# Output projection of an encoder block as seven block products, with sums of the weights kept in DRAM

## The chip, the cores and the metric

The kernel runs on one core of one Trainium2 chip. The metric is device time in microseconds of one execution. TensorE is called PE, VectorE DVE, ScalarE ACT, GpSimd POOL, and SP is the engine that issues most transfers.

## What is computed

The reference is one layer of an encoder with 1024 tokens of width 1024 in float32:

```python
h = jnp.einsum('bsd,de->bse', x, w_in[layer])
q_a, k_a, v_a, z_a, q_b, k_b, v_b, z_b = jnp.split(h, SPLIT_POINTS, axis=-1)
y_a = neighborhood_attention(q_a, k_a, v_a, rel_pos_bias[layer])   # 8 heads of 64, window 8 x 16 in a 16 x 64 grid
qb, kb = rotary(q_b, positions), rotary(k_b, positions)
y_b = windowed_gqa_with_sink(qb, kb, v_b, sink_logits[layer])      # 8 query heads, 2 of keys, |i - j| <= 128
mixed = jnp.concatenate([y_a * jax.nn.silu(z_a), y_b * jax.nn.silu(z_b)], axis=-1)
y = jnp.einsum('bse,ed->bsd', mixed, w_out[layer])
x = layer_norm(DEEPNORM_ALPHA * x + y, ln_gain[layer], ln_bias[layer])
```

(The splitting into heads is left out.) The output projection, `y`, is a product of 1024 x 1024 by 1024 x 1024.

## The kernel before

**Arithmetic.** Products are made in float16 with each operand split in a high and a low part: three passes, high x high, high x low and low x high, are summed in float32 in one PSUM bank of 128 x 512. A split costs a cast on ACT (high part) and a subtraction on DVE or POOL (low part), for weights also a scaling.

**Stages.** First the values are projected, then six of the 21 blocks of 128 columns of the first projection (`project`, L362, with its matmuls at L381). A counter of these matmuls (`run_to`, L390) triggers events at given counts, such as the scans `sum_w` (L700) that read weights for their scale. Then come 128 units of attention, 64 of group b and 64 of group a, one per step. In step i `stage_qk` makes the logits (L799, L800), DVE adds the mask or bias (L809), ACT makes the exponentials (L823) and the high part (L831), DVE the low part (L832), and SP issues a transpose by DMA of both parts (L835). For every four units `stage_pv` multiplies with the values (L861), some steps later. `stage_on` divides, `stage_ot` transposes on PE (L882) and multiplies into the gate `z` (L885, L888). The other 15 projections are fed between the units by `pump_to` (L896) according to the list `FILL_AT`, and after them the first part of the output projection (`out_head`, L1014), 60 matmuls long.

**The order of the work** is the order of the Python calls on each engine: what is written from L571 to L1227 is under a manual schedule. Side work goes through four queues, `enq` and `pop` (L149, L161), one list per engine. In each step `pop` takes a few operations whose inputs were issued in an earlier step (three steps earlier, if the input is a transfer), by priority and then by age: one or more from the list of SP, one or two from ACT's and DVE's, two from POOL's. `need` issues an operation at once if a unit needs it. What follows in `final` (L1025) is ordered by the framework's planner.

**The output projection.** `wo` is loaded in 16 blocks of 128 x 512 (`wo_load`), six of them twice. Every block is scanned for its size in the attention (`wo_scan`: ten on DVE, L939, six on ACT, L936), `wo_scale` (L945) makes one scale, `wo_split` (L955) the parts: eight blocks in the attention, the others in `final`. The gated activations `z` of four of the eight inner blocks (group b) are split by `m_queue` in the attention, the other four in `final`. `out_mms` (L998) makes 3 matmuls per inner block into one bank. `final` first runs what of the second half of row tiles 0 to 2 is ready, then the last four inner blocks for eight banks, then tile by tile. `residual` (L1049) adds a bank to the scaled x (`x_load`, L1043) and gathers statistics, `norm` (L1097) normalizes: one half of the columns on DVE (L1102, L1105), the other on ACT and POOL (L1104, L1107, L1108). The last tile is cut in 256 + 128 + 128 columns and ends in `norm_last` (L1078).

## Time and profile before

| | |
|---|---|
| median of three runs | 447.97 us (447.36 to 450.59) |
| profiled execution | 447.86 us, of which 446.1 us are its span |
| mean granted clock of TensorE | 0.996 |
| busy PE / DVE / ACT / POOL | 438.3 / 346.8 / 302.6 / 211.7 us |
| HBM read / written | 41.19 / 6.32 MB |

Busy times are sums over the whole span; the stages differ. Ends of matmuls are modelled, so that the distance between the starts of matmuls says more than their busy time. In the timeline a row gives the start, the time covered, the engine, the line and what is written from what; in the groups a row gives count, busy time, mean ns of one, and the idle time of the engine before. In the waits a row gives who waited for whom, for how long in total, how often, and the longest. A row of the chain of work gives start, length and what worked.

### The profile page before, as it was taken

The numbers are of one execution on the slowest core, as the hardware profiler recorded it, in microseconds if no ns is written. First come the engines' busy times: TensorE is split into PE (matmuls) and PEld (weight loads), VectorE is DVE, ScalarE is ACT, GpSimd is POOL, SyncE is SP. The second block draws the span as 40 slices with busy tenths as digits, with TensorE's granted clock in tenths as the row PEclk, the third lists the DMA queues.
The fourth block names the chain that finished last, engine by engine and source line by source line (L and its number), as shares of the span: only waits on it lengthen the run. The fifth ranks groups of instructions, "written<-read, shape, count | busy, mean of one in ns | idle before, by whom it ended". The sixth has DMA issues, their size and how long they took to land.

```text
span 446.1 us, 9265 instructions
## 1 busy us (share of the span) xinstructions
PE 438.3 (98%) x3241; PEld 254.7 (57%) x3241; DVE 346.8 (78%) x842; ACT 302.6 (68%) x636; POOL 211.7 (47%) x227
## 2 busy tenths in 40 slices
PE   9999999999999999999999999999999999999995
PEld 8997754444445565655564655555555654444454
DVE  5988867429986797898988887888877737679945
ACT  5849789666599988886867777777777847012411
POOL 0110074636939558767505656655642404304740
PEclk9999999999999999999999999999999999999998
DMA  7921569991149999586876769569569588102711
GB/s 266 391 94 60 164 222 325 278 307 54 48 118 221 188 202 181 95 159 135 168 109 126 144 130 169 112 135 184 116 110 242 108 185 318 48 1 92 238 72 71
DMA packets 123983, 71.20 MB, mean 160 GB/s; under 512 B 96800, under 2 KB 105888, under 8 KB 123936
## 3 DMA queue, kind: packets, MB, share of 16 engines
q1 hardware_dynamic: 123792, 70.48, 65.6%
q8 instruction: 25, 0.41, 0.4%
q14 instruction: 22, 0.18, 0.1%
q10 hardware_dynamic: 144, 0.13, 0.1%
HBM read 41.19 MB, written 6.32 MB: 107 GB/s over the span
## 4 chain that ended last, share of the span: by engine, by line
PE 82%; ACT 5%; DVE 4%; DMA 4%; issue 3%; POOL 1%; SPq 0%; DVEq 0%; POOLq 0%; ACTq 0%
PE ps_pj L381 36%; PE ps_s L1008 9%; PE ps_s L488 6%; PE ps_t L861 6%; PE ps_pj L1008 5%; PE ps_t L1008 5%; PE ps_s L799 3%; PE ps_s L800 3%; PE ps_pj L488 3%; PE ps_t L488 3%; DMA vd<-vt 2%; DMA ws<-in_wt 2%; ACT split L831 1%; PE ps_t L882 1%; DVE qs L257 1%
## 5 line engine op out<-in xcount | busy, mean ns | idle before, releaser
L381 PE MATMUL ps_pj<-xf,wh 128*128 128x512 f16 x672 | 201.3, 379 | 0.9 <-DVE ks L257 0.5
L381 PE MATMUL ps_pj<-xf,wl 128*128 128x512 f16 x336 | 127.3, 379 | 0.0
L381 PEld LDWEIGHTS <-wh 128*128 128x128 f16 x672 | 63.4, 98 | 61.9 <-DVE ks L257 1.3
L823 ACT ACTIVATE ps_s<-sn,nm 128x385 f32<-128x385 f32 (+3 forms) x128 | 70.9, 554 | 29.0 <-DVE nm L809 28.6
L832 DVE SCALAR_TENSOR_TENSOR split<-ps_s,split 128x384 f16<-128x384 f32 (+1 forms) x128 | 66.8, 522 | 30.1 <-ACT split L831 28.4
L1008 PEld LDWEIGHTS <-m 128*128 128x128 f16 x432 | 40.0, 98 | 41.2 <-DVE m L916 0.3
L831 ACT ACTIVATE split<-ps_s 128x384 f16<-128x384 f32 (+1 forms) x128 | 58.6, 458 | 2.4
L381 PEld LDWEIGHTS <-wl 128*128 128x128 f16 x336 | 32.9, 98 | 38.3
L198 POOL TENSOR_SCALAR wr<-wr,wsc 128x512 f32<-128x512 f32 x26 | 20.5, 790 | 66.6 <-ACT wh L193 54.4
L809 DVE CUSTOM_DVE_ANT_0 sn<-ps_s,bm,nsk 128x384 f32<-128x384 f32 (+1 forms) x64 | 40.7, 635 | 0.8 <-PE ps_s L800 0.6
L1008 PE MATMUL ps_s<-wo,m 128*128 128x512 f16 (+1 forms) x192 | 40.7, 366 | 0.0
L799 PE MATMUL ps_s<-ks,qs 128*128 128x384 f16 (+2 forms) x128 | 39.7, 310 | 0.1
L800 PE MATMUL ps_s<-ks,qs 128*128 128x384 f16 (+2 forms) x128 | 39.7, 310 | 0.0
L809 DVE CUSTOM_DVE_ANT_0 sn<-ps_s,bias,sg 128x368 f32<-128x368 f32 (+1 forms) x64 | 36.2, 565 | 3.8 <-PE ps_s L800 3.2
L861 PEld LDWEIGHTS <-tr 128*128 128x128 f16 (+1 forms) x1056 | 36.2, 98 | 2.4
L199 POOL TENSOR_TENSOR wl<-wr,wh 128x512 f16<-128x512 f32 x26 | 32.7, 1256 | 2.2
L299 POOL COPY ks<-ks 64x512 f16<-64x512 f16 x40 | 26.2, 663 | 13.8 <-ACT ks L251 5.2
L1008 PE MATMUL ps_pj<-wo,m 128*128 128x512 f16 (+1 forms) x144 | 26.5, 326 | 0.0
L1107 POOL TENSOR_TENSOR xr<-xr,gb 128x512 f32<-128x512 f32 x7 | 9.8, 1398 | 32.5 <-ACT xr L1104 32.5
L1008 PE MATMUL ps_t<-wo,m 128*128 128x512 f16 x96 | 22.8, 379 | 0.0
L488 PEld LDWEIGHTS <-xf 128*128 128x128 f16 x192 | 18.6, 98 | 7.2
L800 PEld LDWEIGHTS <-qs 128*128 128x128 f16 x128 | 12.5, 98 | 15.5 <-issue 0.8
(190 smaller groups left out, 783.6 us busy)
## 6 DMA issues: line engine op xcount, KB each, us to landing
ws<-in_wt SPq DMA_DIRECT2D x15, 512.0 KB, 6.9
wr<-in_wt SPq DMA_DIRECT2D x26, 256.0 KB, 3.5
wor<-in_wo SPq DMA_DIRECT2D x22, 256.0 KB, 3.3
xr<-in_x SPq DMA_DIRECT2D x8, 512.0 KB, 8.7
out<-xr SPq DMA_DIRECT2D x15, 256.0 KB, 2.0
bias<-in_bias SPq DMA_DIRECT2D x8, 440.0 KB, 3.9
wvraw<-in_wv SPq DMA_DIRECT2D x9, 320.0 KB, 5.8
xraw<-in_xT SPq DMA_DIRECT2D x11, 256.0 KB, 4.4
```

The source lines that it names most:

```text
L199: nc.gpsimd.tensor_sub(l, raw, h)
L299: nc.gpsimd.tensor_copy(place(t, o, half, col), place(t, a, half, col))
L381: nc.tensor.matmul(ps, a[:, k % 4, :], mv, start=(k == 0 and i == 0), stop=(k == KT - 1 and i == 2))
L488: nc.tensor.matmul(ps[:, :320], lh[:, ts], rh[:, cs], start=(k == ko[0] and i == 0), stop=(k == ko[-1] and i == 2))
L799: nc.tensor.matmul(ps[:, :n], q, sl[0], start=True, stop=False)
L800: nc.tensor.matmul(ps[:, :n], q, sl[1], start=False, stop=True)
L809: nc.vector.tensor_tensor_reduce(sn[:, :n], ps[:, :n], bias_t, sg[:, c:c + 1], init, op0=ALU.add, op1=ALU.min, accum_out=nm)
L823: nc.scalar.activation(pt[:, :m], sn[:, :m], AF.Exp, bias=nm, scale=-1.0, accum_out=acc)
L831: nc.scalar.activation(hl[:, :m, 0, :], src, AF.Copy, scale=PSCALE)
L832: nc.vector.scalar_tensor_tensor(hl[:, :m, 1, :], src, PSCALE, hl[:, :m, 0, :], op0=ALU.mult, op1=ALU.subtract)
L861: nc.tensor.matmul(ps[:, w * m:w * m + e], a, b_, start=(i == 0), stop=(i == len(mms) - 1))
L1008: nc.tensor.matmul(ps, lh[:, ts], rh[:, cs], start=(e == EO[0] and i == 0), stop=(e == EO[-1] and i == 2))
```

## The change

The projection is cut in two by two blocks: rows of tokens, inner dimension and columns, each in halves of 512. Seven products of such blocks, q1 to q7 (q4 is called p4), replace the eight. Their left operands are A11, A12, A22 and four sums S1 to S4 of blocks of the gated activations, their right operands B11, B21, B22 and four sums T1 to T4 of blocks of `wo`.

- The scans of `wo` and its scale move from the attention to the loop that projects the values (loads) and to the events of the first six projections (scans and scale).
- `t_prep`, four times in the attention, loads four blocks of `wo` at once, makes T1 to T4, splits them and stores both parts in DRAM (`td`). `t_load` reads them back in `final`. B11, B21 and B22 are loaded, scaled and split as before.
- `m_queue` now splits A11 and S3, the new `m_rest` A12, A22, S1, S2 and S4, for three of the four inner blocks in the attention and for the last in `final`.
- A product is added to banks that already hold another one: q6, q7 and p4 go on top of q1, q3 on top of q5. Between two products `add` adds the bank, with sign + or -, to x (31 additions for 18).
- The list that fills the attention has 57 matmuls of the projection for 60.
- `norm` of all tiles but the last goes through ACT for all 1024 columns and through POOL for gain and bias. All eight tiles of x have a buffer.
- `final` stands under the manual schedule too.

The diff, cut to its core:

```diff
-MSCALE = 2.0 ** -44
+MSCALE = 2.0 ** -46
-LTT, LPP, BH, ND, NA, NX, F1 = 1, 6, 9, 1, 1, 6, 0.2
+LTT, LPP, BH, ND, NA, NX, F1 = 1, 6, 9, 1, 1, 8, 0.2
...
-WO_TAG = ("wor", "wor", "raw", "raw") + ("wr",) * 5 + ("wor", "wor", "raw", "raw", "raw", "wr", "wr")
-WO_SCAN = ((9, 2), (12, 4), (10, 6), (13, 8), (14, 10), (15, 13))
-WO_PREV = {15: ("s", 9), 0: ("s", 10), 1: ("s", 15), 2: ("s", 12), 3: ("s", 13), 11: ("s", 14)}
-WO_SCALE = 55
 M_AT = [105, 112, 118, 120]
-WO_AT = [67, 71, 75, 79, 84, 88, 93, 98]
-WO_LD = [16, 22, 19, 25, 36, 39, 42, 45, 48, 112, 116, 28, 130, 130, 130, 130]
+T_AT = [2, 27, 52, 77]
+B_LD = [36, 39, 42, 45, 48, 70, 78, 87]
+B_AT = [67, 71, 75, 79, 84, 88, 93, 98]
+L_LD = [112, 115, 118, 121]
+L_AT = [126, 128, 130, 132]
+H_AT = [122, 124, 126]
...
+    td = dram.tile([4, 128, 4, 1024], F16, name="td")
...
+        def wo_scan_load(k):
+            for b, w in ((2 * k, "h"), (2 * k + 1, "l")):
+                scans[b] = vw.tile([128, 512], F32, tag=f"wv{w}{k}", name=f"wos{b}")
+                nc.sync.dma_start(scans[b], wo[b // 4, :, b % 4])
+
+        def wo_scan(b):
+            t, m = scans.pop(b), wom[:, b:b + 1]
+            if b % 3 == 2:
+                nc.scalar.activation(t, t, AF.Abs, accum_out=m)
+            else:
+                nc.vector.tensor_reduce(m, t, axis=AXX, op=ALU.add, apply_absolute_value=True)
+
+        def wo_scale():
+            ps = bank("t")
+            nc.tensor.matmul(ps[:, :16], ones, wom.bitcast(BF16)[:, 1::2], start=True, stop=True)
+            nc.vector.tensor_reduce(wog, ps[:, :16], axis=AXX, op=ALU.max)
...
+            nc.vector.tensor_scalar_mul(wos, wos, 0.25)
+            for i in range(2):
+                nc.vector.tensor_scalar(yc[:, i:i + 1], wog, mc, (4.0, -4.0)[i], op0=ALU.mult, op1=ALU.mult)
...
+            wo_scan_load(i)
...
+        for b in range(16):
+            at(18 + 5 * b, wo_scan, b)
         at(219, w_scale, NPRO)
+        at(225, wo_scale)
...
-    rawp = ctx.enter_context(tc.tile_pool(name="rawp", bufs=3, reuse_waits="tile"))
+    rawp = ctx.enter_context(tc.tile_pool(name="rawp", bufs=1, reuse_waits="tile"))
...
-    FILL_N = [48] * len(FILL) + [9, 9, 6, 12, 24]
+    FILL_N = [48] * len(FILL) + [9, 9, 6, 12, 21]
...
+    part, done = {}, {}
+    LHS = {"q1": "A11", "q2": "A12", "q3": "S4", "p4": "A22", "q5": "S1", "q6": "S2", "q7": "S3"}
+    RHS = {"q1": "B11", "q2": "B21", "q3": "B22", "p4": "T4", "q5": "T1", "q6": "T2", "q7": "T3"}
+    ZL, ZH = slice(0, 512), slice(512, S)
+
+    def pair_of(t, *keys):
+        for n, key in enumerate(keys):
+            part[key] = t[:, n, 0, :], t[:, n, 1, :]
...
+    def t_prep(i):
+        raw, hl = {}, {}
+
+        def load():
+            raw[0] = rawp.tile([128, 4, 512], F32, tag="raw", name=f"wor{i}")
+            nc.sync.dma_start(raw[0], wo[i])
+
+        def scale(b):
+            nc.gpsimd.tensor_scalar(raw[0][:, b], raw[0][:, b], wos, 1.0, op0=ALU.mult, op1=ALU.mult)
+
+        def combine(o, fn, a, b):
+            return lambda: getattr(nc.gpsimd, fn)(raw[0][:, o], raw[0][:, a], raw[0][:, b])
+
+        def hi(n, b):
+            if n % 2 == 0:
+                hl[0] = rawp.tile([128, 2, 2, 512], F16, tag="hl", name=f"wohl{i}{n}")
+            nc.scalar.copy(hl[0][:, n % 2, 0], raw[0][:, b])
+
+        def lo(n, b, eng):
+            eng.tensor_sub(hl[0][:, n % 2, 1], raw[0][:, b], hl[0][:, n % 2, 0])
+
+        def store(n):
+            nc.sync.dma_start(td[i, :, n:n + 2], hl[0].rearrange("p b i c -> p b (i c)"))
+
+        ld = enq("sp", load, *t_last)
+        s = [enq("pool", lambda b=b: scale(b), ld) for b in (0, 1, 3, 2)]
+        t1 = enq("pool", combine(0, "tensor_sub", 0, 1), *s[:2])
+        t3 = enq("pool", combine(1, "tensor_sub", 3, 1), t1, s[2])
+        h1 = enq("act", lambda: hi(0, 0), t1)
+        h3 = enq("act", lambda: hi(1, 1), t3, h1)
+        l1 = enq("pool", lambda: lo(0, 0, nc.gpsimd), h1)
+        l3 = enq("dve", lambda: lo(1, 1, nc.vector), h3)
+        w1 = enq("sp", lambda: store(0), l1, l3)
+        t2 = enq("pool", combine(3, "tensor_add", 0, 3), t3)
+        t4 = enq("pool", combine(2, "tensor_sub", 3, 2), t2, s[3])
+        h4 = enq("act", lambda: hi(2, 2), t4, w1)
+        h2 = enq("act", lambda: hi(3, 3), h4)
+        l4 = enq("dve", lambda: lo(2, 2, nc.vector), h4)
+        l2 = enq("pool", lambda: lo(3, 3, nc.gpsimd), h2)
+        t_last[:] = [enq("sp", lambda: store(2), l4, l2)]
+
+    t_last, t_read = [], {}
+
+    def t_load(n, name):
+        t = tiles["fp"].tile([128, 4, 2, 512], F16, name=name, bufs=1)
+        nc.sync.dma_start(t.rearrange("p i h c -> p i (h c)"), td[:, :, n].rearrange("i p c -> p i c"))
+        pair_of(t, *[(name, i) for i in range(4)])
...
+    def m_queue(i):
+        z = zt[4 + i]
+        pair_of(big_tile(f"mb{i}", (128, 2, 2, 512), F16), ("A11", i), ("S3", i))
+        if i == 0:
+            need(*t_last)
+            sums3.append(rawp.tile([128, 4, 512], F32, tag="raw", name="s3"))
+        t = sums3[0][:, i]
+        m_split(("A11", i), z[:, ZL], "pool")
+        o = enq("pool", lambda: nc.gpsimd.tensor_add(t, z[:, ZL], z[:, ZH]))
+        m_split(("S3", i), t, "pool", o)
+
+    def m_rest(i):
+        zb, za = zt[4 + i], zt[i]
+        last = i == 3
...
+        pair_of(a, ("A12", i), ("A22", i))
+        pair_of(c, ("S1", i), ("S2", i))
+        deps = done["A11", i] + done["S3", i] if not last else []
+        add = ("dve", nc.vector) if last else ("pool", nc.gpsimd)
+        s1 = enq(add[0], lambda: add[1].tensor_add(zb[:, ZH], zb[:, ZH], za[:, ZH]), *deps)
+        h12, l12 = m_split(("A12", i), za[:, ZL], "dve" if last else "pool")
+        h22, l22 = m_split(("A22", i), za[:, ZH], "pool")
+        s2 = enq("dve", lambda: nc.vector.scalar_tensor_tensor(
+            zb[:, ZL], zb[:, ZH], -1.0, zb[:, ZL], op0=ALU.mult, op1=ALU.subtract), s1)
+        m_split(("S1", i), zb[:, ZH], "dve", s1)
+        s4 = enq("dve", lambda: nc.vector.tensor_sub(za[:, ZL], za[:, ZL], zb[:, ZL]), s2, l12)
+        m_split(("S2", i), zb[:, ZL], "pool", s2)
+        m_split(("S4", i), za[:, ZL], "dve", s4)
...
+    def prod(name, t, ps, es=range(4), c=(0, 512)):
         o, w = c
...
+        cs = slice(o, o + w)
+        fresh = name in ("q1", "q2", "q5") or c != (0, 512)
+        for i in es:
+            a, b = (LHS[name], i), (RHS[name], i)
+            need(*done.get(a, ()), *done.get(b, ()))
+            (ah, al), (bh, bl) = part[a], part[b]
+            for n, (lh, rh) in enumerate(((ah, bh), (ah, bl), (al, bh))):
+                nc.tensor.matmul(ps[:, cs], lh[:, 128 * t:128 * t + 128], rh[:, cs],
+                                 start=(fresh and i == 0 and n == 0), stop=(i == 3 and n == 2), skip_group_check=True)
                 yield
...
+        t_load(3, "T2")
+        t_load(0, "T1")
...
-        def residual(t, a, ps, c=(0, 512)):
+        def add(t, a, ps, minus, c=(0, 512), whole=False):
             o, w = c
             xv = xrs[t][:, 512 * a + o:512 * a + o + w]
-            nc.vector.scalar_tensor_tensor(xv, ps[:, o:o + w], yc, xv, op0=ALU.mult, op1=ALU.add)
+            nc.vector.scalar_tensor_tensor(xv, ps[:, o:o + w], yc[:, minus:minus + 1], xv, op0=ALU.mult, op1=ALU.add)
...
+            nc.scalar.activation(xr, xr, AF.Identity, bias=nmr, scale=rstd)
+            for h in (slice(0, 512), slice(512, 1024)):
+                nc.gpsimd.tensor_mul(xr[:, h], xr[:, h], gb[:, h])
+                nc.gpsimd.tensor_add(xr[:, h], xr[:, h], bb[:, h])
+                nc.sync.dma_start(out[ts, h], xr[:, h])
...
+        x_load()
+        x_load()
+        m_rest(3)
+        for t in list(xrs):
+            x_scale(t)
+        t_load(1, "T3")
+        t_load(2, "T4")
+        for t in order[:]:
+            x_load()
+            x_scale(t)
+        gb, bb = zslot("gb"), zslot("bb")
+        nc.sync.dma_start(gb, gain.partition_broadcast(128))
+        nc.sync.dma_start(bb, lbias.partition_broadcast(128))
+
+        def run(name, t, ps, *args):
+            list(prod(name, t, ps, *args))
+            return ps
+
+        q, b = obank, [obank["q1", t] for t in range(4)]
+        for name, t, tag in (("q2", 1, "t"), ("q2", 2, "t"), ("q5", 0, "s")):
+            q[name, t] = bank(tag)
+            run(name, t, q[name, t], range(3))
+        add(0, 0, b[0], 0)
+        add(0, 0, run("q2", 0, q["q2", 0], (3,)), 0, whole=True)
+        add(4, 1, run("q5", 0, q["q5", 0], (3,)), 1)
+        add(0, 1, run("q6", 0, b[0]), 0)
+        for t in range(3):
+            if t:
+                q["q5", t] = bank("t")
+                add(4 + t, 1, run("q5", t, q["q5", t]), 1)
+            else:
+                for n in (1, 2):
+                    run("q2", n, q["q2", n], (3,))
+                add(1, 0, b[1], 0)
+                add(1, 0, q["q2", 1], 0, whole=True)
+            add(4 + t, 1, run("q7", t, b[t]), 1, whole=True)
+            if t == 0:
+                add(2, 0, b[2], 0)
+                add(2, 0, q["q2", 2], 0, whole=True)
+            elif t == 1:
+                add(3, 0, b[3], 0)
+            add(t + 1, 1, run("q6", t + 1, b[t + 1]), 0)
+            add(4 + t, 0, run("p4", t, b[t]), 1, whole=True)
+            norm(4 + t)
+            add(t, 1, run("q3", t, q["q5", t]), 0, whole=True)
+            norm(t)
+        ps = run("q5", 3, bank("s"))
+        add(7, 1, ps, 1)
+        add(3, 1, ps, 0)
+        add(7, 1, run("q7", 3, b[3]), 1, whole=True)
+        a = run("q2", 3, bank("pj"), range(2))
+        add(7, 0, run("p4", 3, b[3]), 1, whole=True)
+        add(3, 0, run("q2", 3, a, range(2, 4)), 0, whole=True)
+        norm_ahead(3)
+        norm(7)
+        cuts = [((0, 256), bank("pj")), ((256, 128), None), ((384, 128), None)]
         pn = bank("t")
...
+        for c, ps in cuts:
+            ps = ps or bank("t" if c[0] == 256 else "s")
+            add(3, 1, run("q3", 3, ps, range(4), c), 0, c, whole=True)
+        norm_last(3)
+
+    fill.extend((out_head((0,), range(3), "pj"), out_head((1,), range(3), "pj"),
+                 out_head((0, 1), (3,), None), out_head((2,), range(4), "s"),
+                 out_head((3,), range(4), "s"), out_head((0,), range(3), "s", "q2")))
...
+        if i in T_AT:
+            t_prep(T_AT.index(i))
+        if i in B_LD:
+            n = B_LD.index(i)
+            b_load(n, n // 2, 2 * (n % 2), w_ops.get(21 + n) if n < 5 else b_ops[n - 5])
+        if i in B_AT:
+            n = B_AT.index(i)
+            b_split(n, (("B11", "B21")[n % 2], n // 2), lambda n=n: b_slot(n), "dve" if n % 2 else "pool")
+        if i in L_LD:
+            n = L_LD.index(i)
+            b_load(8 + n, n, 3, b_ops[3 + n])
+        if i in L_AT:
+            n = L_AT.index(i)
+            b_split(8 + n, ("B22", n), lambda n=n: l_slot(n), "pool", *[o for e in range(4) for o in done["S3", e]])
         if i in M_AT:
-            m_queue(4 + M_AT.index(i))
+            m_queue(M_AT.index(i))
+        if i in H_AT:
+            m_rest(H_AT.index(i))
...
     clock["step"] = None
+    final()
     ordered.close()
-    final()
...
-    arr["wo"] = np.ascontiguousarray(np.asarray(inputs["w_out"])[0].reshape(8, 128, 1024))
+    wout = np.asarray(inputs["w_out"])[0].reshape(2, 4, 128, 2, 512)[::-1]
+    arr["wo"] = np.ascontiguousarray(wout.transpose(1, 2, 0, 3, 4).reshape(4, 128, 4, 512))
```

236 lines of the change are left out of this document (63 added, 173 removed).

## The prediction

> **What bounds the kernel now.** I read the page first, then the stretches of the span, then the timeline of the projection at the end, then the waits of the queues that feed the attention.
>
> ```profile
> span 446.1 us, 9265 instructions
> PE 438.3 (98%) x3241; PEld 254.7 (57%) x3241; DVE 346.8 (78%) x842; ACT 302.6 (68%) x636; POOL 211.7 (47%) x227
> PEclk9999999999999999999999999999999999999998
> GB/s 266 391 94 60 164 222 325 278 307 54 48 118 221 188 202 181 95 159 135 168 109 126 144 130 169 112 135 184 116 110 242 108 185 318 48 1 92 238 72 71
> ```
>
> TensorE is busy for 98% of the span at full clock, in every slice but the last. A busy matmul unit need not be a full one, because the ends of matmuls are modelled, so the rate has to be read from starts:
>
> ```profile
> 397.29 5.34 PE L1008 MATMUL ps_pj<-wo,m 128*128 128x512 f16 x24
> 402.47 5.34 PE L1008 MATMUL ps_t<-wo,m 128*128 128x512 f16 x24
> 407.65 5.34 PE L1008 MATMUL ps_pj<-wo,m 128*128 128x512 f16 x24
> ```
>
> These are three row tiles of the output projection. Each begins 5.18 us after the one before, so one matmul of 512 columns takes 5.18 / 24 = 0.2158 us. Nothing lies between the groups. The stretches of the attention look the same (columns: length, then busy us and count of PE, weight loads, DVE, ACT, POOL, then clock, DMA share, GB/s):
>
> ```profile
> 128.00:165.00 37.00, 37.00 (x303) 20.46 (x301) 29.59 (x88) 34.08 (x92) 24.64 (x24) 1.00 0.96 197
> 165.00:195.00 30.00, 30.00 (x269) 17.21 (x267) 26.05 (x74) 24.45 (x61) 23.70 (x26) 1.00 0.88 153
> 195.00:222.00 27.00, 27.00 (x253) 15.65 (x251) 22.73 (x64) 21.77 (x55) 18.74 (x18) 1.00 0.70 146
> 222.00:262.00 40.00, 39.73 (x348) 22.64 (x346) 34.71 (x98) 29.47 (x68) 17.89 (x22) 1.00 0.70 123
> 262.00:292.00 30.00, 30.00 (x269) 17.40 (x267) 25.01 (x66) 23.44 (x48) 18.39 (x22) 1.00 0.76 146
> 318.00:348.00 30.00, 29.63 (x238) 16.22 (x235) 23.70 (x67) 22.70 (x47) 12.16 (x12) 1.00 0.82 163
> 348.00:371.00 23.00, 23.00 (x230) 13.65 (x229) 11.92 (x34) 14.64 (x28) 2.62 (x3) 1.00 0.77 174
> ```
>
> So the kernel is bound by the count of matmuls, from the first projection to the end. A matmul taken away is worth its 0.2158 us only if the other engines keep up, and they have little to spare: DVE is at 80 to 87% and ACT at 74 to 92% in most of these stretches.
>
> **What the change takes from TensorE.** The projection before is 8 row tiles x 2 halves x 8 blocks of the inner dimension x 3 passes = 384 matmuls of 512 columns. After, it is 7 products x 4 row tiles x 4 blocks x 3 passes = 336. The 48 fewer are worth 48 x 0.2158 = **10.4 us**. Three of them leave the list that fills the attention (60 becomes 57), the rest leave the end.
>
> **What it adds in the attention.** Each of the four t_prep steps loads 1 MB of wo and issues on POOL four scalings, four sums and two low parts; on ACT four casts; on DVE two low parts; on SP one load and two stores of 512 KB. The nearest rows for the durations:
>
> ```profile
> L319 POOL TENSOR_TENSOR rp_raw<-rp_raw,rp_sw 128x512 f32<-128x512 f32 x6 | 7.7, 1276 | 0.4
> L198 POOL TENSOR_SCALAR wr<-wr,wsc 128x512 f32<-128x512 f32 x12 | 8.3, 696 | 15.5 <-PE ps_pj L381 6.1 <-PE ps_s L800 5.7 <-ACT wh L193 3.5
> L199 POOL TENSOR_TENSOR wl<-ws,wh 128x512 f16<-128x512 f32 x16 | 18.6, 1160 | 1.3
> L990 ACT CAST m<-z 128x512 f16<-128x512 f32 x8 | 4.5, 608 | 0.0
> L259 DVE TENSOR_TENSOR qs<-rp_raw,qs 64x512 f16<-64x512 f32 x2 | 1.5, 752 | 0.1
> L936 ACT ACTIVATE wor<-wor 128x512 f32<-128x512 f32 x6 | 3.7, 620 | 0.0
> L939 DVE TENSOR_REDUCE wom<-wor 128x1 f32<-128x512 f32 x10 | 6.8, 676 | 1.0 <-DMA wor<-in_wo 1.0
> ```
>
> POOL per t_prep: 4 x 0.70 + 4 x 1.28 + 2 x 1.16 = 10.2 us, 41 us in all. ACT gains 16 x 0.61 = 9.7 us and loses the six scans (3.7 us). DVE gains 8 x 0.75 = 6.0 us and loses ten scans (6.8 us). So ACT and DVE stay about where they are, and POOL takes the load. The steps begin at 2, 27, 52 and 77 of 128, and the sums begin some three steps later, when the load is in. Placed on the stretches: 24.6 + 10.2 = 34.8 of 37 us, 23.7 + 10.2 = 33.9 of 30 us, then 18.7 and the 3.9 left over = 22.6 of 27 us. The third and fourth fall where POOL works 18 of 40 and 18 of 30 us. So POOL runs full from about 131 to 215 us and is some 4 to 8 us behind in places.
>
> POOL itself is not waited for by TensorE at once: low parts of weights and queries are made several steps ahead. What is queued behind it is SP. Each store waits on SP for POOL's low part, and behind it stand the transposes of the attention, one per step, which the product with the values needs:
>
> ```profile
> SPq L182 <- POOL wl L199: 36.1, 10, 6.9
> 146.04 2.54 SPq L835 DMA_TRANSPOSE tr<-split  x2
> 150.27 0.96 PE ps_t L861 x33
> tr<-split SPq DMA_TRANSPOSE x128, 3.1
> wor<-in_wo SPq DMA_DIRECT2D x22, 256.0 KB, 3.3
> ```
>
> The second transpose of the pair starts at 146.04 + 2.54 / 2 = 147.3 us, lands 3.1 us later at 150.4, and the product that reads it starts at 150.27. There the cover is nothing. In exchange the loads of wo for the scans leave this queue (22 loads of wo become 4 large loads, 12 small ones and 8 stores; 16 others go to the front). SP already waits for POOL before, 3.6 us on average, without a gap on TensorE. Bounds for the whole attention: 0 (POOL's lag is swallowed by the steps' lead, as now) and 8 x 1.8 = 14.4 us (every store waits the 3.6 us average and half of it reaches TensorE). It is nearer the lower end, as the 3.6 us waits of today stop nothing and two of the four steps fall where POOL has room: I take **+2.5 us**.
>
> **What it adds at the front.** Sixteen loads of 256 KB (4 MB) go ahead of the attention, with 11 reductions on DVE (7.4 us) and 5 on ACT within pumps 18 to 93 (16 us). They meet this chain:
>
> ```profile
> 70.00:100.00 30.00, 29.69 (x141) 13.36 (x139) 14.43 (x29) 22.80 (x44) 17.02 (x23) 1.00 1.02 302
> 87.54 7.52 DMA ws<-in_wt
> 95.14 1.16 ACT junk L706 x2
> 100.15 7.14 PE ps_pj L381 x33
> ```
>
> DMA is full here, and a load of 7.5 us ends in a scan on ACT that the next weights wait for: no cover. But the wo loads are issued in the loop before, where the GB/s row shows 60 and 164 in the slices from 33 to 56 us, room for 4 MB at 300 GB/s (13 us). Bounds 0 and 4 us (DVE's extra 7.4 us less the gaps it has); I take **+0.5 us**, as DVE is half idle in this stretch.
>
> **The hand-over and the end.** After step 105 POOL gets 4 sums (5.1 us), three m_rest (each 1.28 + 3 x 1.16, 14.3 us) and the four low parts of B22 (7.4 us): 26.8 us against 12.2 + 2.6 us busy of 53. It fits, just. The last z is ready with the last transposes, and its splits (m_rest(3)) are covered by 27 matmuls, 5.8 us:
>
> ```profile
> 370.95 0.60 PE L882 MATMUL ps_t<-identf,on 128*128 128x128 f32 x4
> 371.59 0.75 DVE L888 SCALAR_TENSOR_TENSOR z<-ps_t,zc,z 128x512 f32<-128x512 f32 x1 [3.03 <-PE ps_t L882]
> L1054 DVE SCALAR_TENSOR_TENSOR xr<-ps_s,yc,xr 128x512 f32<-128x512 f32 x7 | 5.2, 737 | 5.4 <-PE ps_s L1008 5.4
> L1047 ACT ACTIVATE xr<-xr 128x1024 f32<-128x1024 f32 x8 | 8.2, 1050 | 1.7 <-DMA xr<-in_x 1.5
> 342.52 19.97 SPq L835 DMA_TRANSPOSE tr<-split  x13
> L1107 POOL TENSOR_TENSOR xr<-xr,gb 128x512 f32<-128x512 f32 x7 | 9.8, 1398 | 32.5 <-ACT xr L1104 32.5
> 439.05 0.35 DVE L1054 SCALAR_TENSOR_TENSOR xr<-ps_pj,yc,xr 128x128 f32<-128x128 f32 x1 [0.66 <-PE ps_pj L1008]
> ```
>
> What is late next is the first bank that is used twice: product six of row tile 0 adds onto the bank of product one, so DVE must first have added that bank to x, and x must be there. Before it on SP's queue stand T2, T1 and two tiles of x, 3 MB. They can start when the last transposes are issued (342.52 + 19.97 = 362.5 us). At the 318 GB/s of the 34th slice they take 9.4 us, at the 185 of the 33rd 16.2 us. Then two scalings (2 x 1.05) and one add (0.74) follow. Product six is due 33 matmuls (7.1 us) after the last transposes, about 378.4. So it is ready at 374.7 or at 381.5: bounds 0 and 3.1 us here, and as much again for x of tile 1 behind T3 and T4: 0 to 6 us. Later, each bank is read by DVE while another product (2.6 us) runs, against 0.74 for the add. Reads of banks rise from 18 to 31, +13 x 0.74 = 9.6 us on DVE, but two DVE passes of each normalization go to POOL: 7 x 2 x 1.40 = 19.6 us more there, 39 us in a tail of 60 us. The last 7.0 us (439.05 to 446.1) stay. I take **+2.0 us**, nearer the lower end, since the end of the attention leaves DMA free.
>
> **Sum.** -10.4 + 0.5 + 2.5 + 2.0 = -5.4 us. The profiled execution took 447.9 us (446.1 of span and 1.8 around it), the same as the median of the runs (447.97). Forecast: **442.5 us**.
>
> **The rivals.**
>
> *Clean.* All added work is hidden, as SP's waits for POOL are today. 447.9 - 10.4 = 437.5 us, with up to 0.5 us less from the scans that leave the attention. Against it: three places without cover (the transposes at 147 us, ws at 95 us, x at the hand-over).
>
> *The end eats the gain.* The loads come late at the hand-over (6 us) and the front loses 2: 447.9 - 10.4 + 2 + 2.5 + 6 = 448.0, no change. For it speaks the DMA share of 0.77 in 348 to 371 us, while transposes still run; against it that x came in time before.
>
> *Slower: SP behind POOL.* t_prep's stores hold SP until POOL has caught up, the transposes go out late, and the product with the values waits. It is one wait for each of the 8 stores. At 1.8 us each it is 14.4 us: 447.9 - 10.4 + 0.5 + 2.0 + 14.4 = 454.4 us. It decides from 12.4 / 8 = 1.55 us per store on (then the loss is over 1%). For it: POOL at 33.9 of 30 us and the longest wait of 6.9 us. Against it: two t_preps fall where POOL has room.
>
> *A wait that slows the clock.* At the very end TensorE has little to do, and the stretch shows what the clock then does:
>
> ```profile
> 420.00:446.00 26.00, 20.60 (x142) 12.04 (x140) 14.80 (x35) 4.27 (x9) 7.92 (x7) 0.94 0.22 84
> ```
>
> A mean of 0.94 over 26 us is 26 x 0.06 / 0.5 = 3.1 us at half clock. If the wait at the hand-over takes its 3.1 us and as long a time at half clock follows, 1.6 us more are lost: 442.5 - 2.0 + 3.1 + 1.6 = 445.2 us. Against it: no wait in the trace is long enough to show it while matmuls still follow. [...]
>
> That the count of matmuls does not fall is excluded by the loops of the diff.
>
> **How the numbers follow.** Clean 0.15, forecast 0.38 (440 to 443.4), the end eats the gain 0.18 (443.4 to 452.4), the slowed clock 0.05, slower 0.24. A measurement of this kernel tells about 1% (4.5 us) from no change. Faster by over 1% is clean and forecast: 0.53; within 1% is the end and the clock: 0.23; slower 0.24. The range goes from clean with its half microsecond, 437.0, into the slow case, 454.0, and leaves out most of that case's upper half; the forecast's own is 440 to 443.4.
>
> **What would show it.** Right: 336 matmuls of 512 columns' worth in the projection; POOL's busy time up by about 41 us in the attention; its gaps gone from 131 to 215 us; attention longer by 1 to 4 us; from the last transposes to the end some 7 us less. Wrong: SP waiting for POOL at the stores for over 3 us each with TensorE idle at the product with the values (slower); gaps over 2 us at product six or at ws; or POOL never behind (clean).

## The result, and the profile after

The changed kernel takes 473.25 us (median of 4 runs, 471.89 to 475.5) against 448.01 us before (447.36 to 450.59): ratio 1.056, interval 1.049 to 1.062. The change makes the kernel slower by 25 us. The forecast was 442.5 us, with a range of 437.0 to 454.0. The execution whose trace is read below took 475.5 us, the longest of the four, 2.2 us above their median.

These lines stand on the page of the changed kernel, whose span is 473.6 us; the last is the share of each engine in the chain that ended last, of which TensorE held 82% before:

```profile
PE 439.5 (93%) x3169; PEld 252.1 (53%) x3169; DVE 362.8 (77%) x855; ACT 319.1 (67%) x662; POOL 287.7 (61%) x297
PEclk9999999999999799999899999899999996999997
PE 48%; DVE 17%; issue 11%; POOL 11%; ACT 7%; DMA 4%; DVEq 0%; SPq 0%; POOLq 0%; ACTq 0%
```

TensorE has gaps and four dents in its clock, where it had none but the end's. Those of its waits that matter below, summed (columns: us in total, times, longest):

```profile
PE ps_t L912 <- DVE on L902: 7.8, 1, 7.8
PE ps_s L829 <- DVE split L862: 5.6, 2, 3.4
PE ps_t L891 <- DMA tr<-split: 3.3, 2, 1.9
PE ps_s L829 <- POOL qs L260: 2.5, 2, 2.2
PE ps_pj L1086 <- DVE xr L1126: 1.3, 1, 1.3
```

Three stretches, of which the two of the attention were full at a clock of 1.00 before (same columns):

```profile
128.00:165.00 37.00, 32.54 (x237) 16.82 (x236) 26.99 (x74) 29.03 (x74) 30.38 (x29) 0.91 0.69 167
195.00:222.00 27.00, 25.50 (x216) 14.20 (x215) 19.20 (x51) 17.69 (x45) 25.87 (x27) 1.00 0.82 162
372.00:400.00 28.00, 19.16 (x166) 11.04 (x165) 20.47 (x40) 15.86 (x31) 25.72 (x21) 0.82 0.76 196
```

From 128 to 165 us TensorE does 237 matmuls where it did 303. Two starts mark the parts: unit 127, the last of the attention, and the last transposes of its output.

```profile
377.99 0.27 PE L829 MATMUL ps_s<-ks,qs 128*128 128x256 f16 x1
400.39 0.60 PE L912 MATMUL ps_t<-identf,on 128*128 128x128 f32 x4
```

Read in the same way for every kernel of this study (us from the start of the span; the last of the four transposes starts 0.3 us after the group; the last matmul of the projection is the last piece of row tile 3):

| kernel | unit 0 | unit 127 | last transpose | last projection matmul | span |
|---|---|---|---|---|---|
| before | 122.0 | 357.2 | 371.3 | 438.8 | 446.1 |
| after | 123.9 | 378.0 | 400.7 | 462.5 | 473.6 |
| no_sums | 123.9 | 368.5 | 390.2 | 452.0 | 463.2 |
| dma_only | 124.4 | 365.4 | 387.8 | 449.6 | 460.7 |
| no_tprep | 124.3 | 359.1 | 381.4 | 443.2 | 454.6 |
| bare | 123.9 | 359.3 | 370.3 | 433.3 | 444.1 |
| order | 122.9 | 377.2 | 400.1 | 461.9 | 473.0 |
| lag | 123.3 | 390.1 | 412.7 | 474.5 | 485.6 |
| split_load | 124.4 | 377.5 | 399.4 | 461.2 | 472.6 |
| rest_dve | 123.1 | 375.9 | 398.9 | 460.7 | 471.8 |
| rest_late | 123.8 | 376.2 | 388.9 | 461.8 | 473.0 |
| rest_quiet | 123.7 | 376.0 | 393.6 | 455.4 | 466.6 |
| norm_dve | 123.6 | 375.1 | 397.4 | 460.2 | 470.4 |
| end_quiet | 124.3 | 377.2 | 399.7 | 461.5 | 470.1 |
| no_scan | 124.2 | 376.8 | 398.3 | 460.1 | 471.2 |

Before to after, part by part: the front +1.9 us; unit 0 to unit 127 254.1 instead of 235.2, +18.9; unit 127 to the last transpose 22.7 instead of 14.1, +8.6; from there to the last matmul 61.8 instead of 67.5, -5.7; the end 11.1 instead of 7.3, +3.8. The sum is 27.5 us, the difference of the spans. Kernels that share a part differ in it: the front by 1.5 us; the attention by 2.6 us in seven kernels in which it is the same but for its last units (251.5 to 254.1, the changed kernel longest); from the last projection matmul to the end by 0.3 us. A smaller difference between two spans says nothing; where a verdict rests on less, it rests on the waits. Each kernel below ran once, except the last, and the kernel before, run beside them, took 448.7 to 451.3 us.

### The profile page after: what moved, and what is told of

The parts are those of the page before. It is cut to its first block, busy times and chain, and to the rows that moved or that the text cites. A ratio compares the mean times of both kernels' runs of the same rounds, so it can differ in the third digit from the quotient of the medians.

```text
span 473.6 us, 9299 instructions
## 1 busy us (share of the span) xinstructions
PE 439.5 (93%) x3169; PEld 252.1 (53%) x3169; DVE 362.8 (77%) x855; ACT 319.1 (67%) x662; POOL 287.7 (61%) x297
## 4 chain that ended last, share of the span: by engine, by line
PE 48%; DVE 17%; issue 11%; POOL 11%; ACT 7%; DMA 4%; DVEq 0%; SPq 0%; POOLq 0%; ACTq 0%
PE ps_pj L382 16%; PE ps_s L489 6%; PE ps_s L1086 5%; PE ps_pj L1086 4%; PE ps_t L891 3%; PE ps_pj L489 3%; PE ps_t L489 3%; DMA tr<-split 3%; PE ps_t L1086 2%; POOL wl L200 2%; ACT split L861 2%; PE ps_s L829 2%; PE ps_s L830 2%; POOL wr L199 2%; DVE split L862 2%
## 5 line engine op out<-in xcount | busy, mean ns | idle before, releaser
L382 PE MATMUL ps_pj<-xf,wh 128*128 128x512 f16 x672 | 204.4, 384 | 1.4 <-DVE z L347 1.0
L382 PE MATMUL ps_pj<-xf,wl 128*128 128x512 f16 x336 | 129.2, 385 | 0.0
L862 DVE SCALAR_TENSOR_TENSOR split<-ps_s,split 128x384 f16<-128x384 f32 (+1 forms) x128 | 66.7, 521 | 37.0 <-ACT split L861 35.6
L829 PE MATMUL ps_s<-ks,qs 128*128 128x384 f16 (+2 forms) x128 | 40.3, 315 | 8.5 <-DVE split L862 5.6
L891 PEld LDWEIGHTS <-tr 128*128 128x128 f16 (+1 forms) x1056 | 37.9, 100 | 6.8 <-DMA tr<-split 4.4
L830 PE MATMUL ps_s<-ks,qs 128*128 128x384 f16 (+2 forms) x128 | 40.3, 314 | 0.0
L1179 POOL TENSOR_TENSOR xr<-xr,gb 128x512 f32<-128x512 f32 x14 | 17.7, 1264 | 25.5 <-ACT xr L1177 25.5
L1138 ACT ACTIVATE sd<-mv,eps 128x1 f32<-128x1 f32 x8 | 2.4, 295 | 35.1 <-DVE mv L1136 35.1
L891 PE MATMUL ps_t<-va,tr 128*128 128x65 f16 (+1 forms) x528 | 20.8, 197 | 3.6 <-DMA tr<-split 3.3
L830 PEld LDWEIGHTS <-qs 128*128 128x128 f16 x128 | 12.7, 99 | 21.3 <-issue 7.3
L829 PEld LDWEIGHTS <-qs 128*128 128x128 f16 x128 | 12.7, 99 | 19.9 <-POOL qs L260 3.8
L805 POOL TENSOR_SCALAR bias<-bias,rsg 128x880 f32<-128x880 f32 x8 | 8.4, 1054 | 20.9 <-DMA bias<-in_bias 20.1
```

The costliest lines, as they stand in the source:

```text
L382: nc.tensor.matmul(ps, a[:, k % 4, :], mv, start=(k == 0 and i == 0), stop=(k == KT - 1 and i == 2))
L829: nc.tensor.matmul(ps[:, :n], q, sl[0], start=True, stop=False)
L830: nc.tensor.matmul(ps[:, :n], q, sl[1], start=False, stop=True)
L862: nc.vector.scalar_tensor_tensor(hl[:, :m, 1, :], src, PSCALE, hl[:, :m, 0, :], op0=ALU.mult, op1=ALU.subtract)
L891: nc.tensor.matmul(ps[:, w * m:w * m + e], a, b_, start=(i == 0), stop=(i == len(mms) - 1))
```

## The experiments

All are the changed kernel with one edit. Three groups: t_prep in the attention, m_rest at the hand-over, and the end with the front; then what remains when all sums are gone.

**t_prep without its sums (no_sums).**

```
-  s = [enq("pool", scale(b), ld) for b in (0, 1, 3, 2)]
-  t1 = enq("pool", combine(0, "tensor_sub", 0, 1), *s[:2])   # and t3, t2, t4
+  t1 = t3 = t2 = t4 = ld
```

> Left out: the four scalings and four sums of each t_prep on POOL (32 of POOL's added operations, 31.7 us); the casts, low parts, load and stores stay and work on the raw blocks, so the products use other data. Theory POOL (results that ACT and TensorE wait for come late because they stand behind t_prep's sums on POOL): the gaps of 2.4 and 2.6 us at units 15 and 16 and of 3.5 us at unit 49 go, with the half clock that follows them (6.8 and 3.4 us); about 473 - 9 - 5 = 459 us. Rival SP (the stores hold the transposes): all eight stores are still there, the gaps stay, 471 to 475. In both the gaps at units 77 to 79 and the 7.9 us at the last transposes stay.

It took 465.04 us, the attention 244.6 instead of 254.1. So the sums and scalings cost 9.5 us there by these two traces, 7 us against the shortest of the kernels with the same attention. How they did it is seen in the changed kernel on ACT and DVE (idle before an instruction and what ended it in brackets):

```profile
150.71 0.62 ACT L254 CAST qs<-rp_raw 64x512 f16<-64x512 f32 x1 [1.55 <-POOL rp_raw L320]
151.75 0.56 DVE L862 SCALAR_TENSOR_TENSOR split<-ps_s,split 128x384 f16<-128x384 f32 x1 [2.88 <-ACT split L861]
221.69 0.69 ACT L346 ACTIVATE z<-ps_pj,invt 128x512 f32<-128x512 f32 x1 [4.05 <-POOL rp_raw L318]
```

In ACT's order a cast of q waited 1.55 us for the rope on POOL (L320), and a tanh 4.05 us for its slot, which POOL's rope still read (L318, the cosine table); the exponentials and high parts came behind them. DVE's split came late (2.88 us idle before the first), the bank of scores was not free, and TensorE waited at its next product with the queries (L829, 2.26 and 3.38 us). Without the sums TensorE waited no longer for POOL at L829, the clock stayed at 1.00 throughout the attention, and two waits of up to 1.9 us for the split were left:

```profile
PE ps_s L829 <- DVE split L862: 3.8, 2, 1.9
```

Theory POOL holds in its mechanism; it had 14 us and the span got shorter by 10.4, since part of the gaps remained. That POOL slows DVE's own operations is not what happens here: from 125 to 357 us the splits of 384 columns (L862, L832 before) take 555 ns in both kernels, the masks of 384 columns 671 and 669, the biases of 368 columns 592 and 594. Of DVE's work there, what is stretched most is t_prep's low parts, with 1.2 us on average (the same operation alone took 0.69 us in the run port below, L59).

**Same work, rope first (order).**

```
-  o3 = enq(eng, ..., o2, after=3)        # rope; likewise o4, o5 and the splits of q and k
+  o3 = enq(eng, ..., o2, prio=0.6, after=3)
```

> Same work as the changed kernel; on POOL the rope, the low parts of q and k and the copies of k go ahead of t_prep's operations when both are ready. Theory POOL, order: the gaps at units 15, 16 and 49 go, about 459 to 463 us. Rival POOL, amount (the queue is simply too full, 34 us of work in 30): the wait moves to t_prep's own casts, which stand in ACT's order ahead of the exponentials, and the attention keeps gaps of the same sum, 468 to 475.

474.76 us. The wait moved as the rival said: ACT now stands at t_prep's own casts, 6.3 us in all instead of 3.0. Its waits for the rope did not go either (8.3 us instead of 6.5).

```profile
151.78 0.62 ACT L960 CAST wohl<-wor 128x512 f16<-128x512 f32 x1 [3.10 <-POOL wor L955]
```

**Same work, consumers of POOL two steps later (lag).**

```
   self.lag = 2 if eng == "sp" else 0
+  if eng == "pool" and clock["step"] is not None and clock["step"] < 100:
+      self.lag = 2
```

> Same work; in steps 0 to 99 whatever uses a result of POOL is issued two steps later than before, so that ACT's and DVE's orders reach it when POOL is done. Theory in-order wait (ACT stands still behind a late result of POOL, with the exponentials behind it, though POOL is busy only 80 to 87% from 125 to 222 us): ACT's waits of 1.6, 3.1 and 4.1 us for POOL go, and with them the gaps at units 15, 16 and 49; 459 to 464 us. Rival amount (POOL's and DVE's work sets the pace): the gaps only move, to the product with queries that come two steps late, 471 to 478.

487.75 us, worse than either theory said. ACT no longer waited for POOL at all, but the low parts of q came too late for TensorE:

```profile
PE ps_s L831 <- POOL qs L262: 15.3, 6, 4.7
```

(L831 is L829 of the changed kernel.) POOL's amount is only part of this. At the waits of 4.7 and 2.7 us POOL works without a gap, but before those of 3.75 and 3.2 us it stands idle until ACT has made the cast of q:

```profile
238.04 1.15 POOL L262 TENSOR_TENSOR qs<-rp_raw,qs 64x512 f16<-64x512 f32 x1 [1.59 <-ACT qs L256]
```

The edit puts off by two steps whatever uses a result of POOL, and starts nothing earlier. So neither another order nor later consumers help; whether an earlier start of the rope would was not tried.

**Loads and stores alone (dma_only), and no t_prep at all (no_tprep).**

```
 dma_only: t_prep keeps    ld = enq("sp", load, *t_last)
                           w1 = enq("sp", store(0), ld);  t_last[:] = [enq("sp", store(2), w1)]
 no_tprep: if i in T_AT: t_prep(...)   is left out; t_load reads vd, same size
```

> Left out of t_prep: everything on POOL, ACT and DVE; its four loads of 1 MB and its eight stores of 512 KB stay, in the same queue, each store behind its load. Theory engines (the casts and low parts in ACT's and DVE's order cost the 8.6 us that remained without the sums): near the kernel without t_prep, 455 to 458. Rival DMA (the transposes stand behind the loads and stores, or land late beside them): near the kernel without the sums, 461 to 465, with gaps at the product with the values that the transposes end.

> Left out: all of t_prep (four loads of 1 MB, POOL's, ACT's and DVE's work on them, eight stores); the loads at the hand-over stay and bring other data of the same size. Theory side work (t_prep is what costs the attention its time): of the 20.8 us by which the last unit starts later than before, only the front's 2 to 3 stay; the hand-over and the end as in the changed kernel; 455 to 457. Rival (the attention loses by the other moved pieces, the loads and splits of B11 and B21 or the shorter list of filling matmuls): 462 or more, little below the 465.0 without the sums.

no_tprep took 456.57 us, and its attention 234.8 us, that of the kernel before (235.2): all of the 18.9 us were t_prep's, with no rest for the other moved pieces. The theory holds. The first stretch is at full clock again, with 312 matmuls:

```profile
125.00:165.00 40.00, 39.31 (x312) 21.46 (x312) 31.89 (x91) 32.74 (x83) 23.19 (x22) 1.00 0.70 127
```

dma_only took 462.72 us, attention 241.0: the loads and stores alone cost 6.2 us. Here the rival DMA holds, and theory engines falls. SP issued one transpose after another at 1.2 to 1.4 us each here, and each load and store took 0.5 to 0.6 us more of it:

```profile
137.93 0.53 SPq L969 DMA_DIRECT2D td<-wor  x1
138.55 1.44 SPq L865 DMA_TRANSPOSE tr<-split  x1
PE ps_t L891 <- DMA tr<-split: 4.5, 3, 1.9
```

The transposes of units 7 and 8 were issued 3 to 4 us after their data was there, and those of units 76 to 78 landed 6 to 8 us after issue. So t_prep's 19.3 us (254.1 - 234.8) split into 6.2 for the transfers, 3.6 for casts and low parts (no_sums less dma_only, 244.6 - 241.0) and 9.5 for POOL's sums. Each share is a difference of two single runs, uncertain by the 2.6 us above, and holds for this order of removal only, since the waits are not independent.

**Four small loads for each large one (split_load).**

```
-  nc.sync.dma_start(raw[0], wo[i])
+  nc.sync.dma_start(raw[0][:, b], wo[i, :, b])    # four steps, one block each
```

> The 1 MB load of each t_prep becomes four loads of 256 KB in four steps; same bytes, same work behind it. Theory burst (the transposes of units 76 to 78 land 8 us after issue because 1 MB, 520 KB of v and the wo blocks are moved together): the landings fall below 6 us, the gaps of 1.6, 2.1 and 0.3 us at units 77 to 79 and the 3.4 us of half clock behind them go, about 467 to 469. Rival total (the DMA engines are full there whatever the pieces, share 0.96 to 0.98 in 292 to 330): gaps of 2 us or more stay, 471 to 475.

474.52 us. What the theory said of the transfers came true: the transposes of units 76 to 78 landed 3.3 to 5.0 us after issue, where those of the changed kernel need about 8, and the longest wait behind them fell from 1.9 to 1.1 us. The gaps of 2 us that the rival expected are not there. The time did not move all the same: the half clock stayed (a mean of 0.79 in 284 to 292 us), and TensorE's waits for POOL at L829 grew from 2.5 to 3.9 us. So the burst is the cause of the late landings, but its removal gained nothing in the total; why the other waits grew is open.

**The hand-over: s1 and A12 on DVE (rest_dve), S2 and S4 after the transposes (rest_late), POOL's part away (rest_quiet).**

```
 rest_dve:   add = ("dve", nc.vector);  m_split(("A12", i), za[:, ZL], "dve")     # all i
 rest_late:  s2, S2, s4, S4 of blocks 0 to 2 issued in final(), behind m_rest(3)
 rest_quiet: for blocks 0 to 2 no s1 and no low part of A12, A22, S2; none of B22
```

> In m_rest(0..2) the sum s1 and the low part of A12 are on DVE instead of POOL, as in m_rest(3): six operations of about 0.7 to 1.2 us more on DVE at the hand-over. Theory wait (DVE, in order, waits there for POOL and with it the last normalization of the product with the values): the gap of 7.9 us at the last transposes falls below 4 us and the half clock behind it shortens, 464 to 468 us. Rival amount (DVE has too much to do there): the gap stays at 7.9 us or grows, 473 to 477.

> The sums S2 and S4 of blocks 0 to 2 with their splits (nine operations on DVE, three on POOL) are issued after the last transposes instead of in steps 122 to 137; all the work is still done. Theory amount and order (DVE, in order, has those nine ahead of the last normalization): the gap of 7.9 us at the last transposes falls below 3 us and the 10.2 us of half clock go; the work now meets the first products of the end, where product six and product three wait for it. If that cover suffices: 460 to 463 us; if the work has no cover there either, a gap of 4 to 8 us at product six: 467 to 471. Rival (the gap comes from POOL's late results, not from DVE's work): the gap stays above 5 us, 472 to 476.

> Left out at the hand-over, for blocks 0 to 2: POOL's part of m_rest (the sum s1 and the low parts of A12, A22 and S2) and the low parts of B22; the products read the high parts twice instead. DVE's nine operations for S1, S2 and S4 stay and so do ACT's casts. Theory stretching and waits (DVE's operations take 1.0 to 1.75 us there instead of 0.68, and it waits 1.6 us for casts and POOL): they go back to 0.7 and the gap of 7.9 us at the last transposes falls to 3 to 4 us, about 466 to 468. Rival number (DVE is late by the nine operations themselves): the gap stays above 6.5 us, 471 to 474.

In the changed kernel DVE comes to the last normalization (L902) through these:

```profile
383.29 1.75 DVE L1069 TENSOR_TENSOR z<-z,z 128x512 f32<-128x512 f32 x1
391.06 1.62 DVE L1069 TENSOR_TENSOR z<-z,z 128x512 f32<-128x512 f32 x1 [1.04 <-POOL ma L1030]
392.81 0.42 DVE L902 TENSOR_TENSOR on<-ps_t,ri 128x256 f32<-128x256 f32 x1
```

The waits of TensorE there, in rest_dve (first row), rest_late (the next two) and rest_quiet (last):

```profile
PE ps_t L912 <- DVE on L902: 9.3, 1, 9.3
PE ps_t L912 <- DVE on L902: 1.5, 1, 1.5
PE ps_pj L1092 <- DVE xr L1132: 10.6, 1, 10.6
PE ps_t L912 <- DVE on L902: 4.2, 1, 4.2
```

rest_dve (473.62 us): with DVE freed from waiting for POOL but given six more operations, the wait grew from 7.8 to 9.3 us. The theory of the wait falls. rest_late (474.77): the wait at the transposes went from 7.8 to 1.5 us and came back at product six, 1.3 to 10.6. The same work, moved, costs the same: it has no cover on either side, and the shorter total that either forecast gave did not come. rest_quiet (468.37): DVE's operations as before (twelve for these blocks), but at 0.68 us each, and L902 starts 10.9 us after unit 127 instead of 14.8. The wait fell to 4.2 us and the hand-over from 22.7 to 17.6 us. So of the 7.8 us, 3.6 are stretching and waits beside POOL; the other 4.2 go with the operations themselves, as rest_late bears out, which moved nine of them with three of POOL's and left 1.5.

**Contention by itself (port).** A kernel of its own: DVE operations on 128 x 512 alone (L53, L55, L57, L63), beside POOL sums (L73, L75, L77, L83), beside POOL scalings (L94).

> A kernel of its own, which computes nothing of the reference: seven kinds of DVE operations four times each, alone, then beside a stream of POOL sums (two inputs), then beside a stream of POOL scalings (one input), then beside ACT. Theory shared access (DVE and POOL shut each other out where DVE takes two inputs from SBUF): operations with two float32 inputs from SBUF go from about 0.68 us to 1.1 or more beside POOL's sums, the small one from 0.16 to 1.0, those with one input from PSUM stay at 0.55 to 0.68; ACT changes nothing. Rival (DVE is slowed by the memory as a whole): all kinds slow down alike, beside ACT too. Rival (the stretches in the kernel are waits that the profile puts into the operation): no kind changes by over 10%.

```profile
L53 DVE TENSOR_TENSOR c<-a,b 128x512 f32<-128x512 f32 x4 | 2.8, 689 | 0.1
L73 DVE TENSOR_TENSOR c<-a,b 128x512 f32<-128x512 f32 x4 | 6.1, 1527 | 0.1
L94 DVE TENSOR_TENSOR c<-a,b 128x512 f32<-128x512 f32 x4 | 3.6, 912 | 0.1
L75 DVE SCALAR_TENSOR_TENSOR c<-a,b 128x512 f32<-128x512 f32 x4 | 6.5, 1633 | 0.1
L57 DVE SCALAR_TENSOR_TENSOR c<-p,b 128x512 f32<-128x512 f32 x4 | 2.8, 691 | 0.1
L77 DVE SCALAR_TENSOR_TENSOR c<-p,b 128x512 f32<-128x512 f32 x4 | 2.8, 691 | 0.1
L63 DVE TENSOR_SCALAR c<-a 128x512 f32<-128x512 f32 x4 | 1.7, 424 | 0.1
L83 DVE TENSOR_SCALAR c<-a 128x512 f32<-128x512 f32 x4 | 5.4, 1341 | 0.1
L69 POOL TENSOR_TENSOR e<-f,g 128x512 f32<-128x512 f32 x5 | 8.0, 1591 | 0.4
L69 POOL TENSOR_TENSOR e<-f,g 128x512 f32<-128x512 f32 x13 | 16.4, 1262 | 1.0
```

The last two rows are POOL's sums while the four operations of L75 run (31.9 to 38.3 us) and when DVE has finished (59 to 75 us). Two inputs from SBUF: 0.69 us alone, 1.53 to 1.63 beside POOL's sums, 0.91 to 0.99 beside its scalings. One input from PSUM (p): 0.691 in both. Beside ACT nothing changed (692). The small operation on 128 x 1 went from 158 to 660 ns, less than the 1.0 us expected. Shared access holds in the rows with two inputs from SBUF and in those with one from PSUM. POOL pays too, but less: a sum takes 1.59 us beside L75 and 1.26 without DVE. That the two shut each other out altogether is not shown: an operation of L75 and a sum beside it took 1.63 and 1.59 us, less than the 1.95 us of one after the other, each at its time alone (0.69 + 1.26), so the two overlap in part.

**The end: the old normalization (norm_dve), no POOL on row tile 7 (end_quiet). The front: no scans (no_scan).**

```
 norm_dve:  first half of a row on DVE (two scalar_tensor_tensor), second on ACT and POOL, as before
 end_quiet: if t != 7: nc.gpsimd.tensor_mul(...), nc.gpsimd.tensor_add(...)
 no_scan:   wo_scan_load and wo_scan left out; wom is set to 1
```

> The normalization of row tiles is put back as in the kernel before (half of its passes on DVE, half on ACT and POOL). Theory POOL at the end: from the last matmul to the end 7.3 us instead of 11.1, about 469.5 us. Rival (the end is held by the added reads of the banks on DVE, which now gets more): no shorter, 473 to 478.

> Left out: POOL's four passes (gain and bias) on row tile 7, the last that POOL normalizes; DVE's work is the same. Theory contention (the last operations of DVE take 1.8, 1.0 and 1.1 us instead of 0.75, 0.16 and 0.57 because POOL reads and writes beside them): these go back, and from the last matmul to the end it is 8 to 8.5 us instead of 11.1, about 470.5. Rival order (DVE comes late because of its adds and statistics): the durations stay, the end within 0.7 us of 11.1.

> Left out: the 16 early loads of wo (4 MB) and the 16 reductions on them; the scale of wo comes from a constant. Theory front (they cost the 1.9 us that the first unit starts late and about 1 us more by unit 4): unit 0 at about 122.0 and the total 470 to 471. Rival (the delay there has another cause, such as the new order of DMAs or the waits for POOL): unit 0 stays within 0.5 us of 123.9.

norm_dve took 472.22 us; from the last matmul to the end 10.2 instead of 11.1, where theory POOL had 7.3, and the tail before it 1.0 us longer: nothing gained, the theory falls. end_quiet took 471.83 us and its end 8.6 us. The last DVE operations, first in the changed kernel, then in end_quiet:

```profile
465.83 1.03 DVE L1145 SCALAR_TENSOR_TENSOR nmr<-mv,rstd 128x1 f32<-128x1 f32 x1
466.79 1.83 DVE L1165 SCALAR_TENSOR_TENSOR xr<-xr,mv,gb 128x512 f32<-128x512 f32 x1
...
464.84 0.16 DVE L1145 SCALAR_TENSOR_TENSOR nmr<-mv,rstd 128x1 f32<-128x1 f32 x1
464.92 0.75 DVE L1165 SCALAR_TENSOR_TENSOR xr<-xr,mv,gb 128x512 f32<-128x512 f32 x1
```

So 2.5 of the end's 3.8 us are contention with POOL. The other 1.3 are probably DVE's added reads of the banks and their order; no run shows it. no_scan took 473.00 us, its unit 0 came at 124.2: the scans cost the front nothing. The theory falls. What ends ACT's idle time is still the arrival of ws:

```profile
96.86 1.06 ACT L732 ACTIVATE junk<-ws 128x1024 bf16<-128x1024 f32 x1 [4.56 <-DMA ws<-in_wt]
```

Unit 0 starts between 122.9 and 124.4 us in all changed kernels, with or without scans; why ws comes later than before is left open.

**All sums gone (bare, bare_timed).** no_tprep, and the left operands are the 16 splits of the kernel before (products five to seven reuse them); the old normalization.

> Left out: t_prep and all sums of the left operands; their splits are the 16 of the kernel before, and products five to seven use blocks that are there; the normalization is that of before. What is left is seven products with their loads and their 31 reads of the banks. Theory (the saving of 10.4 us is real and all else that was lost is the sums and their splits): 447.9 - 10.4 + 2 = 439.5, between 438 and 442. Rival (the order of the end, the T loads or the added reads of the banks cost by themselves): 445 or more.

> The kernel without t_prep and without the sums of the left operands once more, timed in rounds: what the change is worth if its sums cost nothing. By its trace it is 2.0 us shorter in span than the kernel before (444.1 to 446.1): ratio 0.990 to 0.997. If the single run of the kernel before at 451.27 us was the typical one: ratio below 0.99.

bare took 445.97 us, not the 438 to 442 of its theory; the rival, that more than the sums costs, holds. Timed again in turn with the kernel before, it took 446.37 (445.61 to 446.88) against 449.21: ratio 0.9936, interval 0.9919 to 0.9952. Against before (446.1 us of span), unit 127 to the last matmul is 74.0 us instead of 81.6. That is 7.6 saved, with 2.1 us of waits in it for banks that DVE still reads:

```profile
PE ps_pj L1070 <- DVE xr L1110: 1.3, 2, 1.0
PE ps_s L1070 <- DVE xr L1110: 0.8, 1, 0.8
```

So the matmuls taken away are worth 9.7 us here, against 10.4 forecast. The front (+1.9) and the end (10.8 instead of 7.3, +3.5) take most of it. At the end the chain that ended last runs on DVE up to 437.7 us, through adds, statistics and the normalization of row tile 7, while the last projection matmul starts at 433.3. This bounds the change: with this front and end, sums and their splits at no cost at all would gain 0.6%. Cheaper sums were not tried for that reason; whether front and end could be mended is open.

## Why the prediction was wrong

The gain was right; the costs were not.

- **The saving, -10.4 us:** right. From the last transpose to the last matmul it is 5.7 us less, 1.4 us of wait at product six included, so 7.1 us for 33 matmuls; the other 15 lie before.
- **Attention, +2.5 us: 18.9** (16 to 19 with the spread of that part). The step that failed is "POOL itself is not waited for by TensorE at once", and with it "POOL's lag is swallowed by the steps' lead, as now". The place was right in part (POOL at 25.87 of 27 us in 195 to 222, but at 23.6 of 30 in 165 to 195, where 33.9 had been counted), the follower was wrong: not SP at the stores but ACT, which has casts of POOL's results ahead of the exponentials. SP waited at the stores once:

```profile
SPq L966 <- POOL wohl L963: 1.0, 1, 1.0
```

  So the slower rival was right in its sign and wrong in its mechanism, and the bound of 14.4 us, made from SP's waits, held nothing. What the prediction did not price at all is SP's own time for the loads and stores, 6.2 us in dma_only. The rows for that were there: transposes 1.27 us apart with a cover of nothing.
- **"ACT and DVE stay about where they are": wrong as a price.** In the whole kernel the busy time of DVE grew by 16.0 us and that of ACT by 16.5. DVE's added rows were priced at 0.75 us from a row on 64 partitions. They took 0.68 to 1.75 us. The kernel before had shown it in its normalization, in the first of two passes of DVE with the same shape: three of its seven operations ran beside POOL's passes and took 1.49 to 1.71 us, the other four 0.74 to 0.75:

```profile
L1102 DVE SCALAR_TENSOR_TENSOR xr<-xr,mv,gb 128x512 f32<-128x512 f32 x7 | 7.7, 1100 | 0.1
L1105 DVE SCALAR_TENSOR_TENSOR xr<-xr,rstd,bb 128x512 f32<-128x512 f32 x7 | 5.2, 742 | 0.0
```

- **Hand-over and end, +2.0 us: 17.0.** 8.6 more up to the last transpose, though 15 matmuls fewer (3.2 us) lie there, is 11.8 lost; 1.4 at product six (I had 0 to 3.1 for it); 3.8 at the end. I looked for what is late in DMA and found x; late was DVE, by m_rest's sums and splits. "It fits, just" was counted for POOL alone; the twelve operations that m_rest puts on DVE before the last transposes were given no term. "The last 7.0 us stay" failed by POOL's passes beside DVE's last ones.
- **Front, +0.5 us: 1.9,** inside its bounds, but not by the scans.
- **The slowed clock** was put at 5% and at one place. It came at four:

```profile
153.00:161.00 8.00, 5.80 (x47) 2.77 (x46) 7.01 (x18) 6.18 (x16) 7.61 (x8) 0.57 0.65 132
389.00:400.00 11.00, 6.62 (x49) 4.20 (x50) 5.39 (x8) 2.94 (x5) 10.60 (x10) 0.54 0.92 335
```

  A mean of 0.57 over 8 us is 8 x 0.43 / 0.5 = 6.9 us at half clock (the clock read 0.50 from 153.6 to 160.0 us), by estimate 3.4 us lost if TensorE was otherwise busy. The rival's "as long a time at half clock follows" had no row behind it; here 6.4 us at 0.50 stood beside waits of 2.26 and 2.20 us. This dent is partly chance: six other kernels with two much like waits there (1.6 to 2.1 and 1.9 to 2.5 us) had a mean of 0.91, 0.96, 0.96, 1.00, 1.00 and 1.00 over 125 to 165 us, the changed kernel 0.91.

With the measured terms, -10.4 + 1.9 + 18.9 + 17.0 = 27.4 us, against 27.5 between the spans.

## What to carry to other kernels

Where TensorE is full and the others are at 75 to 90%, price a change by what it adds to the others, each in its order: for every result of a slow engine ask which engine has the consumer in its queue, and what stands behind that consumer. Then price DVE's operations with two inputs from SBUF by what runs on POOL beside them (here 0.69 us became 1.53 to 1.63 beside sums and 0.91 to 0.99 beside scalings), or give them an input from PSUM (0.69 us here, alone and beside POOL). And before working on a cheaper way to do the added work, run the kernel without it: here that bound was 0.6%.
